# First group of an input projection: x's first tiles by another queue, products in the order of their parts

## The chip, the cores and the metric

One core of a Trainium2 chip. The metric is the device time of one execution in microseconds (us), the median of several runs. TensorE (PE) multiplies 128x128 weights with up to 512 columns into PSUM; ScalarE (ACT) and VectorE (DVE) work elementwise; GpSimd (POOL) sets a few constants; SyncE (SP) issues transfers. Each engine executes its own instructions in order and waits on semaphores for the others.

## What is computed

One decoder layer on x of 256 tokens by 1024: a root-mean-square norm, one input projection into queries, keys and values of two head groups, block attention and gated linear attention (GLA) on them, an output projection, a gated convolutional feed-forward block, and a last norm. The part around the change is the first of the projections, GLA's q and k and the 16 columns of its gate:

```python
xn = rms_norm(x, attn_norm_g[l])
proj = xn @ w_in[l]
...
gq = split_heads(proj[..., o_gq:o_gk], GLA_HEADS)
gk = split_heads(proj[..., o_gk:o_gv], GLA_HEADS)
gate_lr = proj[..., o_gg:]
log_a = jax.nn.log_sigmoid((gate_lr @ w_gate_up[l] + b_gate[l]).astype(jnp.float32)) / GLA_GATE_TAU
```

The norm's factor of a token is applied behind the products, so the products start from x itself.

## The kernel before, in words

Every 32-bit product is made of three products of split numbers: each operand is a high part (hi, rounded to the matmul's type) and a low part (lo, the rest), and hi·hi, hi·lo and lo·hi are added up (`mm3`, lines 108 to 111). ScalarE makes a high part (`split_hi`, L92), VectorE the low part from it (`split_lo`, L95). For x the two are `ah` and `al` (`xsplit`, L169 and L170); for weights `hi` and `lo`.

Weights come in slots. A slot is a tile `raw` that a transfer fills (four buffers), and a pair hi and lo (three buffers each). The low part that ends a slot calls `load_next`, which issues the next slot's transfer into the buffer just freed. Slots 0 to 3 hold the first group's weights, two depth steps k of 528 columns each; slots 4 and up hold 512 columns for four depth steps.

The input projection runs over 48 steps q: group g = q // 8 and depth step k = q % 8. Group 0 (G, q = 0 to 7) is GLA's q, k and gate columns: 256 tokens in two halves tt, 528 columns in two parts (272 and 256, one PSUM bank each), three products: 12 a step, 96 in all, lines 658 to 667. Group 1 and 2 (q, k of the attention) have 12 products of 256 columns a step.

Which work stands at which step is a plan: `on(q, f)` puts f ahead of step q's products (lines 558 to 626). TensorE's order is the written one. ScalarE's and VectorE's instructions are put in order by the scheduler, by what it expects to be ready first. In the plan `xsplit(k)` stands at q = k-1; the squares of x (`xsq`, L232) and their sum (`xadd`, `xsum`) at q = 1 to 8; the norm's factor (`xnorm`, L246 on TensorE, then Ln and Exp, L177 and L178) at q = 8; its row (`xrow`, L254), the evacuation of group 0 (`g_evac`, L262 and L263) and the split of the gate columns (`g_lr_split`) at 10; transposes (L282, L291) at 11; the gate's products (L311) at 12; its decay at 14; the gate's weights (`g_wgs`, L268 and L270) at 8. Slot 1's and later slots' splits start up to seven steps ahead of their use.

All of x and the weights are issued by SP, in this order: x k=0, slot 0 in three parts with x k=1 behind the second, x k=2, slot 1's half, x k=3, slot 1's other half, x k=4-5, slot 2, x k=6-7, slot 3. Small constants (wgu, ident, par, cos, sin) are issued at q = 1 to 4 among the later slots' transfers.

Ahead of the first product TensorE runs six warming products of zeros (L73, each two instructions), and ScalarE loads its function table (L54).

Of the kernel before, what the change touches and what calls it, by code (L numbers as in the profile page):

```python
# [9 lines left out]
F32 = mybir.dt.float32  # L10
# [8 lines left out]
HM, HD = 8, 64  # L19
HG, DK, DV = 4, 64, 128  # L20
RANK = 16
WARM = 6
TAU = 16.0
DFF = 2816
NP = DFF // 128
# [9 lines left out]
def trunk_kernel(ctx: ExitStack, tc: tile.TileContext, xT_d, wG_d, w5_d, wo_d, up_d, dn_d,  # L35
# [15 lines left out]
        return ps_att.tile([128, 512], F32, name="att")  # L51


    A.preload_act_table_set("natural_log_exp_and_others")  # L54
    par = const.tile([128, NPAR], F32, name="par")
    cos = const.tile([128, S], F32, name="cos")
    sin = const.tile([128, S], F32, name="sin")
# [11 lines left out]
    warm = const.tile([128, 128], F32, name="warm")  # L69
    V.memset(warm, 0.0)  # L70
    wp = att()
    for _ in range(WARM):
        T.matmul(wp[:, :128], warm, warm, start=True, stop=True)  # L73


    RAW, SPL = 4, 3
# [55 lines left out]
    def load_next():  # L132
        if nload[0] < len(items):
            items[nload[0]].load()
            nload[0] += 1
# [9 lines left out]
    rsx = main.tile([128, 8], F32, name="rsx")  # L145

    slots[0].raw = ring.tile([128, 2048], F32, name="raw", bufs=RAW)
    def load_x(k0, k1):
        a, b = (KT + S * k0 if k0 else 0), KT + S * k1
        DMA.dma_start(xg[:, a:b], xT_d[:, a:b])  # L150

    load_x(0, 1)
    for a, b in ((0, 272), (272, NG), (NG, 2 * NG)):
        DMA.dma_start(slots[0].raw[:, a:b], slots[0].src[:, a:b])
        if b == NG:
            load_x(1, 2)
    nload[0] = 1
    load_x(2, 3)
    slots[1].raw = ring.tile([128, 2048], F32, name="raw", bufs=RAW)
    DMA.dma_start(slots[1].raw[:, :NG], slots[1].src[:, :NG])  # L160
    load_x(3, 4)
    DMA.dma_start(slots[1].raw[:, NG:2 * NG], slots[1].src[:, NG:])
    nload[0] = 2
    for s in range(2, 4):
        load_x(2 * s, 2 * s + 2)
        load_next()

    def xsplit(k):
        A.activation(ah[:, k], xT[:, k], AF.Copy, scale=pag[:, k:k + 1])  # L169
        V.scalar_tensor_tensor(al[:, k], xT[:, k], pag[:, k:k + 1], ah[:, k],  # L170
                               op0=ALU.mult, op1=ALU.subtract)
# [59 lines left out]
    def xsq(n):  # L231
        A.activation(xsqs[:, 2 * n:2 * n + 2], xT[:, 2 * n:2 * n + 2], AF.Square)  # L232
# [325 lines left out]
    def on(q, f, *a):  # L558
        plan.setdefault(q, []).append((f, a))

    for k in range(1, KT):
        on(k - 1, xsplit, k)
    for dst, src, q in ((wgu, wgu_d, 1), (ident, ident_d, 1), (par, par_d, 3), (cos, cos_d, 4),
                        (sin, sin_d, 4), (lvl, lvl_d, 10), (causal, causal_d, 14), (glag, gla_g_d, 24)):
        on(q, DMA.dma_start, dst, src)
    for n in range(4):
        on(2 * n + 1, xsq, n)
        if n:
            on(2 * n + 1, xadd, n)
    on(8, xsum)  # L570
    on(8, xnorm)
    on(10, xrow)
    for tt in range(2):
        on(16, rope_a, 0, tt)
        on(24, rope_a, 1, tt)
    on(10, g_evac, 0)
    on(10, g_evac, 1)
    on(8, g_wgs)
    on(10, g_lr_split)
    on(11, g_transpose_lr)  # L580
    on(11, g_transpose, 0)
    on(11, g_transpose, 1)
    on(16, g_diag)
    on(12, g_gate_mm)
    on(12, g_gate)
    on(14, g_decay)
    on(15, lvl_u, 0)
    on(19, lvl_u, 1)
    on(24, lvl_first)
# [26 lines left out]
    for tt in range(2):  # L616
        on(53 + tt, g_out, tt)

    for n, sl in enumerate(slots[1:], 1):
        q0 = first_use[n]  # L620
        qa = max(0, q0 - 7)
        if n >= SPL:
            qa = max(qa, first_use[n - SPL + 1])
        on(qa, sl.alloc)
        on(qa, sl.split, 0, sl.n // 2)
        on(qa + (3 if q0 - qa > 4 else 1), sl.split, sl.n // 2, sl.n)

    slots[0].alloc()
    xsplit(0)
    for a, b in ((0, 272), (272, NG), (NG, 2 * NG)):  # L630
        slots[0].split(a, b)

    def emit(q):
        for f, a in plan.get(q, []):
            f(*a)

    names = ["G", "q", "k", "v", "gv", "r"]
    for q in range(48):
        g, k = divmod(q, 8)
        emit(q)  # L640
        if k == 0:
            if g == 0:
                st["G"] = [(acc(), att()) for _ in range(2)]
            else:
                st[names[g]] = [acc() for _ in range(2)]
        if g == 0:
            h_, l_ = slots[k // 2].view(NG)
            kk = k % 2
        else:
            h_, l_ = slots[4 + 2 * (g - 1) + k // 4].view(512)  # L650
            kk = k % 4
        if g in (1, 2):
            for pr in range(4):
                cs = slice(pr * 128, pr * 128 + 128)
                mm3(st[names[g]][pr // 2][:, (pr % 2) * S:(pr % 2 + 1) * S], h_[:, kk, cs], l_[:, kk, cs],
                    ah[:, k], al[:, k], k == 0 and pr % 2 == 0, k == KT - 1, skip_group_check=True)
            continue
        for tt in range(2):
            sh = ah[:, k, tt * 128:(tt + 1) * 128]
            sl = al[:, k, tt * 128:(tt + 1) * 128]  # L660
            if g == 0:
                a, b = st["G"][tt]
                parts = ((a[:, :272], 0, 272), (b[:, :256], 272, 528))
            else:
                parts = ((st[names[g]][tt], 0, 512),)
            for o, c0, c1 in parts:
                mm3(o, sh, sl, h_[:, kk, c0:c1], l_[:, kk, c0:c1], k == 0, k == KT - 1)


    hh_ = main.tile([128, KT, S], F32R, name="hh", tag="ah")  # L670
# [385 lines left out]
```

## Time and profile before

| | us |
|---|---|
| median of 3 runs | 314.3 (314.22 to 314.69) |
| profiled execution, its own time | 314.39 |
| its span, first to last instruction | 311.8 |
| TensorE busy | 304.9 (98%) |
| VectorE busy | 246.0 (79%) |
| ScalarE busy | 201.5 (65%) |
| first to last product of the first group | 4.18 to 19.19 |

The profile is of one execution, with times from the start of its span. A product's duration is modelled and overlaps its neighbour's, so the distance from start to start is what to read. Idle time in a row is what its engine stood still ahead of it, and behind the arrow is what ended that. L92 is line 92 of the kernel.

### The profile page before, as it was taken

The page shows a single profiled execution, that of the slowest core. Times are in us where ns is not written, and L with a number is a line of the kernel's source. Part 1 is how long each engine was busy: PE and PEld are TensorE (multiplying, and loading weights), DVE is VectorE, ACT ScalarE, POOL GpSimd, SP SyncE. Part 2 cuts the span into 40 slices and gives each one's busy share as a digit, 9 for nine tenths or more (in the row PEclk, how much of TensorE's full clock was granted, in tenths as well). Part 3 has the DMA queues.
Part 4 walks back from the last instruction along what each step waited for, and adds up shares of the span by engine and source line. Part 5 has one row for each costly group of instructions (what it writes and reads, how often), then busy time and mean ns, then how long its engine had stood idle before and what let it go on. Part 6 is the DMA issues. An engine that isn't in the chain of part 4 may idle for free.

```text
span 311.8 us, 6135 instructions
## 1 busy us (share of the span) xinstructions
PE 304.9 (98%) x2458; PEld 282.9 (91%) x2458; DVE 246.0 (79%) x464; ACT 201.5 (65%) x367; POOL 1.8 (1%) x12
## 2 busy tenths in 40 slices
PE   8999999999999999999999999999999999999992
PEld 7999997776788999999999999999999999999982
DVE  3996989897747497999999878888777777776653
ACT  5989997588866486466766655566666555534362
POOL 1000000000000000000000000000000000000000
PEclk9999999999999999999999999999999999999999
DMA  6998733734430615694566654445455722220003
GB/s 185 386 407 326 297 131 154 271 111 161 137 137 24 246 41 193 229 372 181 203 212 232 266 210 172 163 183 193 195 203 204 269 67 69 67 69 0 2 0 135
DMA packets 12443, 55.38 MB, mean 178 GB/s; under 512 B 1392, under 2 KB 3200, under 8 KB 8064
## 3 DMA queue, kind: packets, MB, share of 16 engines
q1 hardware_dynamic: 12272, 54.75, 47.5%
q8 instruction: 19, 0.31, 0.4%
q10 hardware_dynamic: 144, 0.26, 0.2%
q14 instruction: 8, 0.07, 0.1%
HBM read 53.95 MB, written 1.05 MB: 176 GB/s over the span
## 4 chain that ended last, share of the span: by engine, by line
PE 96%; DMA 1%; ACT 1%; DVE 0%; SPq 0%; issue 0%; DVEq 0%; ACTq 0%
PE acc L109 15%; PE acc L110 15%; PE acc L111 15%; PE att L110 15%; PE att L109 15%; PE att L111 15%; DMA xg<-in_xT 1%; PE att L377 1%; PE att L536 1%; PE att L506 1%; PE att L548 1%; PE att L439 1%; PE acc L816 0%; PE att L437 0%; PE att L470 0%; PE att L549 0%
## 5 line engine op out<-in xcount | busy, mean ns | idle before, releaser
L92 ACT ACTIVATE hi<-raw 128x1024 fp32r<-128x1024 f32 (+3 forms) x84 | 79.7, 973 | 51.0 <-PE att L110 43.2
L95 DVE TENSOR_TENSOR lo<-raw,hi 128x1024 fp32r<-128x1024 f32 (+3 forms) x86 | 93.6, 1099 | 12.6 <-ACT hi L92 12.5
L109 PE MATMUL att<-hh,hi 128*128 128x256 f32 x352 | 98.5, 280 | 0.0
L111 PE MATMUL att<-hh,lo 128*128 128x256 f32 x352 | 98.4, 279 | 0.0
L110 PE MATMUL att<-hl,hi 128*128 128x256 f32 x352 | 98.3, 279 | 0.0
L109 PEld LDWEIGHTS att<-hh,hi 128*128 128x128 f32 x352 | 66.2, 188 | 0.0
L111 PEld LDWEIGHTS att<-hh,lo 128*128 128x128 f32 x352 | 66.2, 188 | 0.0
L110 PEld LDWEIGHTS att<-hl,hi 128*128 128x128 f32 x352 | 66.2, 188 | 0.0
L782 DVE SCALAR_TENSOR_TENSOR c<-us,par,c 128x256 f32<-128x256 f32 x88 | 40.7, 482 | 4.1 <-ACT c L774 2.5
L774 ACT ACTIVATE c<-us,par 128x256 f32<-128x256 f32 x44 | 24.0, 591 | 21.5 <-DVE us L764 16.0
L111 PE MATMUL acc<-dhi,gl 128*128 128x512 f32 (+1 forms) x88 | 32.3, 367 | 0.0
L110 PE MATMUL acc<-dlo,gh 128*128 128x512 f32 (+1 forms) x88 | 32.2, 366 | 0.0
L109 PE MATMUL acc<-dhi,gh 128*128 128x512 f32 (+1 forms) x88 | 31.8, 361 | 0.0
L721 DVE TENSOR_TENSOR dlo<-draw,dhi 128x1024 fp32r<-128x1024 f32 x22 | 26.6, 1219 | 0.0
L764 DVE TENSOR_TENSOR us<-att,rb 128x512 f32<-128x512 f32 x20 | 13.8, 689 | 15.9 <-PE att L111 15.9
L109 PE MATMUL acc<-hi,ah 128*128 128x512 f32 (+1 forms) x64 | 25.6, 400 | 0.2 <-ACT hi L92 0.2
L110 PE MATMUL acc<-lo,ah 128*128 128x512 f32 (+1 forms) x64 | 24.6, 384 | 0.1
L111 PE MATMUL acc<-hi,al 128*128 128x512 f32 (+1 forms) x64 | 24.2, 378 | 0.0
L716 ACT ACTIVATE dhi<-draw 128x1024 fp32r<-128x1024 f32 x22 | 23.1, 1048 | 0.0
L110 PEld LDWEIGHTS acc<-dlo,gh 128*128 128x128 f32 x88 | 16.5, 188 | 3.0
L109 PEld LDWEIGHTS acc<-dhi,gh 128*128 128x128 f32 x88 | 16.6, 188 | 2.9
L111 PEld LDWEIGHTS acc<-dhi,gl 128*128 128x128 f32 x88 | 16.5, 188 | 2.6
(202 smaller groups left out, 517.3 us busy)
## 6 DMA issues: line engine op xcount, KB each, us to landing
raw<-in_up SPq DMA_DIRECT2D x22, 1024.0 KB, 4.8
draw<-in_dn SPq DMA_DIRECT2D x22, 512.0 KB, 5.7
raw<-in_w SPq DMA_DIRECT2D x8, 1024.0 KB, 6.8
raw<-in_wo SPq DMA_DIRECT2D x4, 1024.0 KB, 4.8
raw<-in_w SPq DMA_DIRECT2D x4, 512.0 KB, 7.3
raw<-in_wG SPq DMA_DIRECT2D x2, 528.0 KB, 6.9
raw<-in_wG SPq DMA_DIRECT2D x3, 264.0 KB, 4.3
xg<-in_xT SPq DMA_DIRECT2D x2, 256.0 KB, 6.0
```

The source lines that it names most:

```text
L92: A.activation(self.hi[:, a:b], self.raw[:, a:b], AF.Copy)
L95: V.tensor_sub(self.lo[:, a:b], self.raw[:, a:b], self.hi[:, a:b])
L109: T.matmul(out, sh, mh, start=first, stop=False, **kw)
L110: T.matmul(out, sh, ml, start=False, stop=False, **kw)
L111: T.matmul(out, sl, mh, start=False, stop=last, **kw)
L377: T.matmul(p[h][64 * j:64 * j + 64, c + 32 * g:c + 32 * g + 32], k[ps, a:a + 64], q, start=True, stop=True)
L439: T.matmul(o, AT[:, i], gv[:, tt, vs], start=(tt == 0), stop=True)
L716: A.activation(hi, downs[i][0], AF.Copy)
L721: V.tensor_sub(lo, d, hi)
L764: V.tensor_tensor(u[:, :, 2:], upo[i][2].rearrange("p (a t) -> p a t", a=2), rb[:, None, :].to_broadcast([128, 2, S]), op=ALU.mult)
L774: A.activation(cv[i][:, a], u[:, a, 2:], AF.Identity, bias=par[:, P_CB + m:P_CB + m + 1], scale=par[:, P_CW + 2 * 2 * NP + m:P_CW + 2 * 2 ...
L782: V.scalar_tensor_tensor(c[:, a], u[:, a, w:w + S], par[:, wc:wc + 1], c[:, a], op0=ALU.mult, op1=ALU.add)
```

## The change

ScalarE's queue issues x of k=0 and k=1 and loads the table behind them; SP issues the weights of slot 0 at once and then whole pairs of x and whole slots, the constants behind slot 3. VectorE copies the first 272 columns of the first high part. From there to q = 14 ScalarE's and VectorE's instructions stand in the written order. A step's twelve products of the first group go by part: four hi·ah, four hi·al, four lo·ah. Norm, row, transposes and gate stand up to one step later, wgs at 11; there are seven warming products.

```diff
-WARM = 6
+WARM = 7
...
-    A.preload_act_table_set("natural_log_exp_and_others")
...
+    with tc.manual_schedule(engines={mybir.EngineType.Activation}):
+        load_x(A, 0, 1)
+        load_x(A, 1, 2)
+        A.preload_act_table_set("natural_log_exp_and_others")
     for a, b in ((0, 272), (272, NG), (NG, 2 * NG)):
         DMA.dma_start(slots[0].raw[:, a:b], slots[0].src[:, a:b])
-        if b == NG:
-            load_x(1, 2)
     nload[0] = 1
-    load_x(2, 3)
-    slots[1].raw = ring.tile([128, 2048], F32, name="raw", bufs=RAW)
-    DMA.dma_start(slots[1].raw[:, :NG], slots[1].src[:, :NG])
-    load_x(3, 4)
-    DMA.dma_start(slots[1].raw[:, NG:2 * NG], slots[1].src[:, NG:])
...
+    load_x(DMA, 2, 4)
+    load_next()
+    load_x(DMA, 4, 6)
+    load_next()
+    load_x(DMA, 6, 8)
+    load_next()
+    for dst, src in ((ident, ident_d), (cos, cos_d), (sin, sin_d), (par, par_d), (wgu, wgu_d)):
+        DMA.dma_start(dst, src)
...
+    first = ExitStack()
+    first.enter_context(tc.manual_schedule(engines={mybir.EngineType.Activation, mybir.EngineType.DVE}))
+
+    def gsplit(k):
+        sl, a = slots[k // 2], NG * (k % 2)
+        if k % 2 == 0:
+            sl.alloc()
+        xsplit(k)
+        if k == 1:
+            xsq(0)
+        sl.split(a, a + NG)
+
     slots[0].alloc()
+    V.tensor_copy(slots[0].hi[:, :272], slots[0].raw[:, :272])
     xsplit(0)
-    for a, b in ((0, 272), (272, NG), (NG, 2 * NG)):
-        slots[0].split(a, b)
+    slots[0].split_hi(272, NG)
+    slots[0].split_lo(0, 272)
+    slots[0].split_lo(272, NG)
+    for k in range(1, 5):
+        gsplit(k)
+    xsq(1)
+    gsplit(5)
+
+    def first_group(q):
+        if q == 2:
+            gsplit(6)
+            xsq(2)
+            xadd(1)
+            gsplit(7)
+            xsq(3)
+            xadd(2)
+        elif q == 4:
+            slots[4].alloc()
+            slots[4].split(0, 1024)
+            xadd(3)
+            xsum()
+            slots[4].split(1024, 2048)
+        elif q == 6:
+            slots[5].alloc()
+            slots[5].split_hi(0, 1024)
+            slots[5].split_hi(1024, 2048)
+        elif q == 9:
+            xnorm()
+            slots[5].split_lo(0, 1024)
+            g_evac(0)
+            g_evac(1)
+            g_lr_split()
+            slots[6].alloc()
+            slots[6].split_hi(0, 1024)
+            slots[5].split_lo(1024, 2048)
+        elif q == 11:
+            xrow()
+            g_wgs()
+        elif q == 12:
+            g_transpose_lr()
+            g_transpose(0)
+            g_transpose(1)
+            slots[6].split_hi(1024, 2048)
+            slots[6].split_lo(0, 1024)
+        elif q == 13:
+            g_gate_mm()
+            g_gate()
+        elif q == 14:
+            g_decay()
+            slots[6].split_lo(1024, 2048)
+            first.close()
...
         emit(q)
+        first_group(q)
...
+        if g == 0:
+            for n, (mov, sta) in enumerate(((h_, ah), (h_, al), (l_, ah))):
+                for c, (c0, c1) in enumerate(((0, 272), (272, 528))):
+                    for tt in range(2):
+                        T.matmul(st["G"][tt][c][:, :c1 - c0], sta[:, k, tt * 128:(tt + 1) * 128],
+                                 mov[:, kk, c0:c1], start=k == 0 and n == 0, stop=k == KT - 1 and n == 2)
+            continue
```

The plan's lines for what `first_group` now calls are taken out, and the plan's loop over slots starts at slot 7.

## Rows read from the trace of the kernel before

**Rows 1.** The page of the profile: the line of busy time by engine (busy us, share of the span, instructions; PE is TensorE's products, PEld its weight loads), and the shares by engine in the chain of work that ended last.

```profile
PE 304.9 (98%) x2458; PEld 282.9 (91%) x2458; DVE 246.0 (79%) x464; ACT 201.5 (65%) x367; POOL 1.8 (1%) x12
...
PE 96%; DMA 1%; ACT 1%; DVE 0%; SPq 0%; issue 0%; DVEq 0%; ACTq 0%
```

**Rows 2.** Busy time by stretch, the long middle of the span. Columns: stretch and its length, busy us and instructions of TensorE, its weight loads, VectorE, ScalarE and GpSimd, then the granted TensorE clock, the DMA engines' mean share and GB/s.

```profile
30.00:300.00 270.00, 270.00 (x2220) 249.68 (x2220) 219.71 (x409) 171.67 (x310) 0.32 (x3) 1.00 0.45 164
```

**Rows 3.** The same view for the last 36 products of the first group.

```profile
14.81:19.19 4.38, 4.38 (x38) 4.38 (x37) 4.38 (x7) 4.19 (x7) 0.00 (x0) 1.00 1.07 420
```

**Rows 4.** TensorE's products in order of time, 0 to 10.5 us. Columns: start us, duration us, engine, line, operation, output <- inputs, shapes, count, and in brackets the idle time before and what ended it.

```profile
1.05 2.93 PE L73 MATMUL att<-warm 128*128 128x128 f32 x12 [1.05 <-DVE warm L70]
4.18 0.60 PE L109 MATMUL acc<-hi,ah 128*128 128x272 f32 x1 [0.20 <-ACT hi L92]
4.73 0.59 PE L110 MATMUL acc<-lo,ah 128*128 128x272 f32 x1
...
5.35 0.41 PE L109 MATMUL att<-hi,ah 128*128 128x256 f32 x1
...
6.44 0.43 PE L111 MATMUL acc<-hi,al 128*128 128x272 f32 x1
...
7.31 0.50 PE L109 MATMUL acc<-hi,ah 128*128 128x272 f32 x1
7.96 0.60 PE L110 MATMUL acc<-lo,ah 128*128 128x272 f32 x1
...
9.90 0.35 PE L109 MATMUL att<-hi,ah 128*128 128x256 f32 x1
```

**Rows 5.** ScalarE in order of time, the same columns: the start of the span, and its late table load and its one issue of a transfer. Two hi in one row start half the way apart (12.91 - 11.83 is two of them).

```profile
3.30 0.51 ACT L169 ACTIVATE ah<-xg 128x256 fp32r<-128x256 f32 x1 [1.29 <-DMA xg<-in_xT]
...
11.83 1.18 ACT L92 ACTIVATE hi<-raw 128x528 fp32r<-128x528 f32 x2
12.91 0.89 ACT L169 ACTIVATE ah<-xg 128x256 fp32r<-128x256 f32 x2
13.71 0.62 ACT L232 ACTIVATE xsqs<-xg 128x512 f32<-128x512 f32 x1
...
20.42 0.26 ACT L177 ACTIVATE rsx<-att,eps 128x2 f32<-128x2 f32 x1 [1.05 <-DVE rsx L176]
...
299.15 1.28 ACT L948 ACT_TABLE_LOAD   x1
300.75 0.60 ACT L974 ACTIVATE jk<-acc 128x512 f32<-128x512 f32 x1 [0.32 <-PE acc L111]
...
308.43 0.39 ACTq L994 DMA_DIRECT2D out_y<-yy  x1
```

**Rows 6.** SP's queue in order of time: its fifth issue, and the two of slot 5 (x2: two issues in one row).

```profile
2.57 0.43 SPq L154 DMA_DIRECT2D raw<-in_wG  x1
...
11.34 0.81 SPq L85 DMA_DIRECT2D raw<-in_w  x2
```

**Rows 7.** Transfers by issue: destination <- source, queue, number, KB, us from the start of the issue to landing. In order, those issued at 0.73 (x, k=0), 3.52 and 4.47 (slot 1, k=2 and k=3), 5.42 (slot 2, whole), 7.93 and 8.36 (slot 4's halves) and 11.8 (slot 5's second half). Slot 3's stood at 6.37.

```profile
xg<-in_xT SPq DMA_DIRECT2D x1, 132.0 KB, 2.5
...
raw<-in_wG SPq DMA_DIRECT2D x1, 264.0 KB, 4.3
...
raw<-in_wG SPq DMA_DIRECT2D x1, 264.0 KB, 5.1
...
raw<-in_wG SPq DMA_DIRECT2D x1, 528.0 KB, 6.4
...
raw<-in_w SPq DMA_DIRECT2D x1, 512.0 KB, 7.2
...
raw<-in_w SPq DMA_DIRECT2D x1, 512.0 KB, 8.2
...
raw<-in_w SPq DMA_DIRECT2D x1, 512.0 KB, 7.4
```

**Rows 8.** VectorE in order of time.

```profile
4.24 0.77 DVE L95 TENSOR_TENSOR lo<-raw,hi 128x272 fp32r<-128x272 f32 x2
...
11.22 0.88 DVE L170 SCALAR_TENSOR_TENSOR al<-xg,ah 128x256 fp32r<-128x256 f32 x2
...
12.62 1.32 DVE L95 TENSOR_TENSOR lo<-raw,hi 128x528 fp32r<-128x528 f32 x2
...
16.82 1.22 DVE L95 TENSOR_TENSOR lo<-raw,hi 128x1024 fp32r<-128x1024 f32 x1
...
23.35 0.20 DVE L276 CAST lrs<-gqk 128x64 fp32r<-128x64 f32 x1 [0.22 <-ACT gqk L262]
```

**Rows 9.** Busy time by stretch again, for the DMA engines (the last two columns).

```profile
6.50:8.00 1.50, 1.35 (x7) 1.04 (x6) 0.93 (x3) 1.20 (x4) 0.00 (x0) 1.00 0.65 195
...
10.00:12.00 2.00, 2.00 (x18) 2.00 (x18) 2.00 (x4) 2.00 (x5) 0.00 (x0) 1.00 1.03 411
```

**Rows 10.** TensorE's products behind the first group: the norm, the product after it, and the transposes.

```profile
19.19 0.50 PE L246 MATMUL att<-ones,s 128*128 128x1 f32 x4
19.55 0.36 PE L109 MATMUL acc<-ah,hi 128*128 128x256 f32 x1
...
24.29 0.38 PE L282 MATMUL att<-ident,lrs 128*128 128x128 f32 x2
24.51 1.04 PE L291 MATMUL att<-ident,gqk 128*128 128x128 f32 x8
```

More of the change, by code (lines that the diff above doesn't have):

```diff
@@ L71, in trunk_kernel, with warming @@
     wp = att()
-    for _ in range(WARM):
-        T.matmul(wp[:, :128], warm, warm, start=True, stop=True)
+    def warming(n, w):
+        for _ in range(n):
+            T.matmul(wp[:, :w], warm, warm[:, :w], start=True, stop=True)
+    warming(WARM, 128)
     RAW, SPL = 4, 3
@@ L147, in trunk_kernel, with load_x @@
     slots[0].raw = ring.tile([128, 2048], F32, name="raw", bufs=RAW)
-    def load_x(k0, k1):
+    def load_x(q, k0, k1):
         a, b = (KT + S * k0 if k0 else 0), KT + S * k1
-        DMA.dma_start(xg[:, a:b], xT_d[:, a:b])
-    load_x(0, 1)
+        q.dma_start(xg[:, a:b], xT_d[:, a:b])
+    with tc.manual_schedule(engines={mybir.EngineType.Activation}):
+        load_x(A, 0, 1)
+        load_x(A, 1, 2)
+        A.preload_act_table_set("natural_log_exp_and_others")
     for a, b in ((0, 272), (272, NG), (NG, 2 * NG)):
         DMA.dma_start(slots[0].raw[:, a:b], slots[0].src[:, a:b])
-        if b == NG:
-            load_x(1, 2)
     nload[0] = 1
-    load_x(2, 3)
-    slots[1].raw = ring.tile([128, 2048], F32, name="raw", bufs=RAW)
-    DMA.dma_start(slots[1].raw[:, :NG], slots[1].src[:, :NG])
-    load_x(3, 4)
-    DMA.dma_start(slots[1].raw[:, NG:2 * NG], slots[1].src[:, NG:])
[L163 to L166, printed above, removed]
+    load_x(DMA, 2, 4)
[6 more added lines that the diff above has]
+        DMA.dma_start(dst, src)
     def xsplit(k):
@@ L559, in on @@
         plan.setdefault(q, []).append((f, a))
[L561 to L564, printed above, removed]
+    for dst, src, q in ((lvl, lvl_d, 10), (causal, causal_d, 14), (glag, gla_g_d, 24)):
         on(q, DMA.dma_start, dst, src)
[L566 to L572, printed above, removed]
     for tt in range(2):
@@ L575, in trunk_kernel @@
         on(24, rope_a, 1, tt)
[L576 to L582, printed above, removed]
     on(16, g_diag)
-    on(12, g_gate_mm)
-    on(12, g_gate)
-    on(14, g_decay)
     on(15, lvl_u, 0)
@@ L617, in trunk_kernel @@
         on(53 + tt, g_out, tt)
-    for n, sl in enumerate(slots[1:], 1):
+    for n, sl in enumerate(slots[7:], 7):
         q0 = first_use[n]
@@ L660, in trunk_kernel @@
             sl = al[:, k, tt * 128:(tt + 1) * 128]
[L661 to L667, printed above, removed]
+            mm3(st[names[g]][tt], sh, sl, h_[:, kk], l_[:, kk], k == 0, k == KT - 1)
     hh_ = main.tile([128, KT, S], F32R, name="hh", tag="ah")
```

## The prediction

> **What bounds the kernel now.** I read four views, in this order. The page's summary [rows 1] says TensorE is the end: it is busy 98% of the span and holds 96% of the chain that ended last. A share over the whole span does not say where time can be had, so next the stretches: between 30 and 300 us TensorE is busy all 270.00 of 270.00 us [rows 2]. Nothing there waits, so TensorE's products simply follow one another, and what is saved ahead of them moves the end by the same amount. That leaves the start. There the reader is to see three losses [rows 3, 4]: first a stretch of the group at its best pace, then its products one by one. First, the products of the first group (8 depth steps k of 12 products, 96 in all) run from 4.18 us to 19.19, where the norm's follow [rows 4, 10], 15.01 us, while the last 36 of them take 4.38 us, 0.1217 us each; at that pace 96 would take 11.7 us. Second, holes: product 2 comes 0.55 us after product 1, because it wants the low part of the weights, and at k=1 product 2 comes 0.65 us after product 1 for the same reason (idle before, released by VectorE's lo). Third, the pace: from 5.35 to 6.44 us five steps take 1.09 us, 0.218 us each, and the change to 0.12 comes near 9.9 us. 256 columns at 1.2 and 2.4 GHz are 0.213 and 0.107 us, so these are the two levels of the clock; the granted-clock column reads 1.00 already there and does not show it, the products' spacing does. Before the rise TensorE had run warming products from 1.05 us, then the first group with its two holes.
>
> **The terms, part by part.** The sum is made against the profiled execution: span 311.8 us, own time 314.39, so 2.6 us lie around the span; it is 0.09 us above the median 314.30.
>
> *Seven warming products.* Six are 12 instructions from 1.05 us; they end at 3.98 with the last lasting 0.43, so 0.23 us each [rows 4]. Fourteen hold TensorE until 1.05 + 14 x 0.23 = 4.27. The first product in the written order needs only ah of k=0 and the first 272 columns of hi. ah: x's first tile lands 2.5 us after its issue and ScalarE takes 0.51 [rows 5, 7], so 0.73 + 2.5 + 0.1 + 0.51 = 3.8, as before. hi: the weights are now SP's first issue, land about then too, and VectorE copies them; no row shows a copy of 272 columns, the bounds are the CAST of 64 columns, 0.20, and the subtraction of 272, half of 0.77 [rows 8]; with 0.3 it is there at 3.6. Both lie under the warming, which now sets the first product: 4.27, **0.09 later** than before.
>
> *x by ScalarE's queue, table load behind it.* ScalarE's only row of an issue lasts 0.39 us, and SP's fifth issue stood at 2.57 [rows 5, 6], so that one comes every 0.46. So ScalarE issues x0 at 0.73, x1 at 1.17, loads the table from 1.6 to 2.9, and x0 lands at 3.2: cost nothing, covered by that landing; without this cover up to 1.7 us of ah0. The late table load lasts 1.28 us, and the next ACTIVATE starts 0.32 us after it, with a matmul named as its releaser [rows 5]. The Trainium skill ("ScalarE: Activation LUTs", What ACT_TABLE_LOAD costs) says otherwise: 1.28 us and then some 1.38 us of drain, 2.66 in all. By that rule ah0 would start at 4.3 and the first product at 4.85; the late row disagrees, 1.60 us from the load's start to the next instruction.
>
> *Written order in parts.* Per k the four hi.ah products come first, then four hi.al, then four lo.ah: lo is wanted eight products after hi, not one. lo of k=0 is there by 5.0, wanted at 4.27 + 8 x 0.218 = 6.0. So both holes go. Weight loads do not increase: every product has a load of its own already [rows 1].
>
> *DMA order.* SP now issues w0 in two parts, w1, x2-3, slot 1 whole, x4-5, slot 2, x6-7, slot 3, then five constants: slot 1 fifth, at 2.57 instead of 3.52 and 4.47, slot 3 ninth, at 4.47 instead of 6.37 [rows 6, 7]. What becomes late next is k=2, which wants slot 1. In the kernel before the last 264 KB of slot 1 were 5.1 us in flight, its first 264 KB 4.3, and slot 2's 528 KB 6.4 [rows 7]; so slot 1 lands between 6.9 and 9.0. I take 7.9, near the row with the same 1,572 KB issued up to it (2.57 + 5.1 = 7.7). hi of k=2 is then out at 7.9 + 0.1 + 0.64 = 8.65. The Trainium skill ("DMA: Bandwidth & Descriptors", Issuing engines are not separate DMA queues) says that a second issuing engine saves only issue time. By this rule x1 wins nothing but its two places in SP's queue; the sum counts no more than that, though the DMA engines stood at 0.65 busy from 6.5 to 8.0 us before [rows 9], when SP had issued everything up to slot 3.
>
> *When the clock rises* no row of before can say for another stream of products. Bounds: the start of before's unbroken products, 5.1 us, and the same moment, 9.9. The stream is now unbroken from 1.05 on, and 5.1 is a bound without a rise in any row, so I take a moment past the middle, nearer to 9.9: **8.0**.
>
> *The first group.* From 4.27 to 8.0 at 0.218 are 17.1 products; the other 78.9 at 0.1217 take 9.60 us: end **17.6** instead of 19.19, 1.59 us earlier. k=2 starts at 8.0 + 6.9 x 0.1217 = 8.84, after 8.65: no hole. The other engines keep up: per pair of k ScalarE wants 1.08 for two hi, 0.80 for two ah and 0.62 for the squares, 2.5 us, and VectorE 0.88 for two al, 1.32 for two lo and as much as one lo for adding the squares, 2.9 at most, since neighbours overlap [rows 5, 8], against 24 x 0.1217 = 2.9.
>
> *Behind it, in written order.* Three thin covers. Slot 4's lo: ScalarE works through from hi of k=2 at 8.0 to hi of slot 4 at about 16.0, VectorE subtracts, 1.22 [rows 8], until 17.3; wanted at 17.9. Constants now travel ahead of slot 4: 64 + 128 + 128 + 93 + 16 = 429 KB by their tiles, at 411 GB/s [rows 9] about 1.0 us. Slot 4's halves landed at 7.9 + 7.2 = 15.1 and 8.4 + 8.2 = 16.6 [rows 7]; 1.9 sooner with slot 3 and 1.0 later makes 14.3 and 15.7, and ScalarE comes to them at 15.0 and 16.0. The norm and the gate: Ln now stands behind the high part of slot 5's second half in ScalarE's queue. That half landed at 11.8 + 7.4 = 19.2 before [rows 6, 7]; the stream is 1.9 us ahead and has 349 KB more in front, as wgu and ident went ahead of it already (0.9 us), so 18.2; its high part lasts 1.0, and Ln starts at 19.5. From Ln to the transposes it took 24.29 - 20.42 = 3.87 us [rows 5, 10]: 23.4. TensorE comes there at 17.6 + 4 x 12 x 0.1217 + 2 x 0.36 (the norm, 19.19 to 19.55, and the row taken alike) = 24.2. The gate's weights wgs: ScalarE ends the evacuations at 22.7, slot 6's high part at 23.7 and its two copies at 24.5; VectorE has a low part until 24.6, cos and sin and two subtractions of some 0.4 each: 26.2. TensorE wants them after the transposes (1.2 us) and twelve products, at 26.8. From both sides the three are 0 to 0.5 us, no gain being possible behind a TensorE that is not kept waiting; I take **0.1**. Nothing else gets longer: the norm, row, transposes and gate are the same instructions a step later.
>
> **Sum:** -1.59 + 0.1 = -1.5 us; 314.39 - 1.5 - 0.09 = **312.8**. Its own range: clock at 6.5 with slot 1 at 6.9 ends the group at 4.27 + 2.23 + 85.8 x 0.1217 = 16.9, 312.0; clock at 9 ends it at 18.0, 313.3.
>
> **The rivals.**
> *A. The clock rises at the same moment, 9.9.* Then 25.8 products go at the slow pace and the group ends at 18.4: only holes are won, -0.65, 313.65. For it: nothing in the trace ties the rise to the holes. Against: the products ran unbroken in before only from 5.1 on, now from the start.
> *B. Slot 1 as one transfer lands at 9.0* (slot 2's 6.4 us) or as late as slot 1 was whole before, 9.57. k=2 then starts at 9.7 or 10.3 and the group ends at 18.5 to 19.1: 313.7 to 314.2, no change. For it: halves became a whole and share the engines with more bytes; against: issued 0.95 and 1.9 us sooner.
> *C. Slower: ScalarE's written order.* Ln, the evacuations and the gate wait behind a high part that waits for slot 5's second half. It decides from a landing of 19.2 on (19.2 + 0.1 + 1.0 + 3.87 = 24.2); each us later costs one, and past 21.3 the 1.5 are gone and 0.6 more: 315 to 316. For it: before, ScalarE's order was not fixed and a late high part could be stepped over; against: 18.2 by the landings.
> *D. The table load holds ScalarE as the page says:* first product 0.6 us later, the group that much later: 313.4. The late row speaks against it.
>
> **Numbers.** A change of 0.2%, 0.63 us, is about the least that can be told here (the three runs spread over 0.47); faster means under 313.67. Forecast 0.56, A 0.22 (half of it on either side of that line), B 0.11 (mostly no change), C 0.08, D 0.03. Faster 0.56 + 0.11 + 0.03 + 0.02 = 0.72, same 0.20, slower 0.08. The range leaves out C and the far ends of B and of the early clock: 311.9 to 313.9.
>
> **What would show it.** Right: first product at 4.2 to 4.4 with no idle TensorE before it; eight products of k=0 and k=1 without a wait for lo; spacing falling to 0.12 before 9.0; slot 1 landing near 7.9; last product of the first group near 17.6; TensorE busy throughout from 30 on. Wrong: spacing of 0.22 until 9.9 (A); a wait of TensorE at k=2 for hi, released by a transfer (B); TensorE waiting at the transposes or the gate products for evacuations whose ScalarE queue waits on slot 5 (C); ah0 after 4.0 without a late landing (D). If the first group ends near 17.6 and the time does not follow, then the later stretch was not as tight as it looks.

## The result: slower by 2.2 us

The kernel after takes 316.4 us (median of 8 runs, 315.15 to 318.02); the one before, beside it, 314.24 (8 runs). The ratio is 1.0071, 95% interval 1.0054 to 1.0088: slower, and 2.5 us above the upper end of the range, 313.9. The profiled execution took 316.94 with a span of 315.2, so 1.74 us lie around the span, where before had 2.59. The span alone grew by 3.4 us, and the time around it fell by 0.85. The three longest of the eight executions (317.06 to 318.02) are those with the lowest mean granted clock, 0.993 to 0.994 against 0.998 in the other five (315.15 to 316.94), and the profile shown is of one of the five; four executions lie at 315.15 to 315.86 and four at 316.94 and above, with the median between them.

### The profile page after: what moved, and what is told of

Same layout as the page of the kernel before. It is cut to its first block, busy times and chain, and to the rows that moved or that the text cites. A ratio compares the mean times of both kernels' runs of the same rounds, so it can differ in the third digit from the quotient of the medians.

```text
span 315.2 us, 6135 instructions
## 1 busy us (share of the span) xinstructions
PE 305.4 (97%) x2460; PEld 283.5 (90%) x2460; DVE 246.7 (78%) x465; ACT 201.7 (64%) x366; POOL 1.8 (1%) x12
## 4 chain that ended last, share of the span: by engine, by line
PE 94%; ACT 2%; DMA 1%; DVE 1%; issue 0%; DVEq 0%; SPq 0%; ACTq 0%
PE acc L112 14%; PE att L114 14%; PE att L113 14%; PE att L112 14%; PE acc L114 14%; PE acc L113 14%; PE att L713 2%; PE acc L713 2%; DMA raw<-in_wG 1%; PE att L381 1%; PE att L540 1%; PE att L510 1%; ACT qs L487 1%; PE att L552 1%; PE att L443 1%; PE acc L868 0%
## 5 line engine op out<-in xcount | busy, mean ns | idle before, releaser
L114 PE MATMUL acc<-ah,lo 128*128 128x256 f32 x64 | 18.0, 281 | 2.5 <-DVE lo L98 2.5
L112 PE MATMUL acc<-hi,ah 128*128 128x512 f32 x48 | 20.2, 421 | 0.0
L114 PE MATMUL acc<-hi,al 128*128 128x512 f32 x48 | 19.0, 396 | 0.0
L113 PE MATMUL acc<-lo,ah 128*128 128x512 f32 x48 | 19.0, 396 | 0.0
```

What stands on the lines that cost most here:

```text
L112: T.matmul(out, sh, mh, start=first, stop=False, **kw)
L113: T.matmul(out, sh, ml, start=False, stop=False, **kw)
L114: T.matmul(out, sl, mh, start=False, stop=last, **kw)
```

## The profile after

First the page's line of busy time by engine and the shares of the chain that ended last, then the stretch 30 to 300 us; they answer to [rows 1, 2].

```profile
PE 305.4 (97%) x2460; PEld 283.5 (90%) x2460; DVE 246.7 (78%) x465; ACT 201.7 (64%) x366; POOL 1.8 (1%) x12
...
PE 94%; ACT 2%; DMA 1%; DVE 1%; issue 0%; DVEq 0%; SPq 0%; ACTq 0%
```

```profile
30.00:300.00 270.00, 267.53 (x2212) 247.85 (x2211) 220.04 (x408) 172.98 (x311) 0.31 (x3) 1.00 0.46 166
```

TensorE now stands still for 2.47 us of a stretch where it never did. TensorE's products in order of time show where (answers to [rows 4, 10]).

```profile
1.05 3.35 PE L74 MATMUL att<-warm 128*128 128x128 f32 x14 [1.05 <-DVE warm L69]
4.43 0.82 PE L713 MATMUL acc<-hi,ah 128*128 128x272 f32 x2
5.41 0.79 PE L713 MATMUL att<-hi,ah 128*128 128x256 f32 x2 [0.15 <-ACT hi L95]
...
9.52 0.66 PE L713 MATMUL acc<-lo,ah 128*128 128x272 f32 x2
9.97 0.52 PE L713 MATMUL att<-lo,ah 128*128 128x256 f32 x2
10.33 0.41 PE L713 MATMUL acc<-hi,ah 128*128 128x272 f32 x2
...
18.85 0.40 PE L713 MATMUL att<-lo,ah 128*128 128x256 f32 x2
20.48 0.50 PE L250 MATMUL att<-ones,s 128*128 128x1 f32 x4
24.27 0.68 PE L258 MATMUL att<-ident,rsx 128*128 128x128 f32 x4 [0.37 <-issue]
28.80 0.47 PE L315 MATMUL att<-lrT,wgs 128*128 128x256 f32 x2
...
38.97 0.38 PE L114 MATMUL acc<-ah,lo 128*128 128x256 f32 x1 [2.47 <-DVE lo L98]
```

The holes for lo are gone, but a row of two products still takes 0.45 us until 9.97: the clock rose at 10.0, as in before. The group ends at 19.08, 0.11 us sooner than [rows 4, 10]. The first GLA block's products, at 43.91 before, stand at 47.33: 3.4 us are lost between the two points, and nothing after. The rows show 0.37 and 2.47 us of it as idle of TensorE. SP's queue shows the first reason (answers to [rows 6]; the last row holds the two halves of slot 4, of slot 5, and three more).

```profile
3.87 0.33 SPq L88 DMA_DIRECT2D raw<-in_wG  x1
...
7.50 0.33 SPq L170 DMA_DIRECT2D sin<-in_sin  x1
8.88 0.33 SPq L170 DMA_DIRECT2D par<-in_par  x1
9.54 0.34 SPq L170 DMA_DIRECT2D wgu<-in_wgu  x1
10.97 10.27 SPq L88 DMA_DIRECT2D raw<-in_w  x7
```

Slot 1, issued at 2.58, was 6.3 us in flight and landed at 8.88, when `par` was issued; slot 2, issued at 3.87, was 7.0 in flight and landed at 10.87, and slot 4 went out at 10.97. SP waits for the oldest transfer: eight are in flight (ScalarE's two counted in), and an issue goes out when the eighth before it has landed. Slot 4 is issued 3.0 us later than in before (7.93), and slot 5's second half lands at 13.4 + 8.7 = 22.1. ScalarE in order of time (answers to [rows 5]):

```profile
0.73 0.89 ACTq L153 DMA_DIRECT2D xg<-in_xT  x2
1.66 1.28 ACT L159 ACT_TABLE_LOAD   x1 [1.66 <-PEq L1097]
3.87 0.51 ACT L173 ACTIVATE ah<-xg 128x256 fp32r<-128x256 f32 x1 [0.93 <-DMA xg<-in_xT]
...
22.14 1.06 ACT L95 ACTIVATE hi<-raw 128x1024 fp32r<-128x1024 f32 x1 [1.56 <-DMA raw<-in_w]
23.10 0.24 ACT L181 ACTIVATE rsx<-att,eps 128x2 f32<-128x2 f32 x1
```

The Ln at 23.10 stood at 20.42: it waits behind that high part. TensorE pays 0.37 us of it at 24.27. Last, VectorE ahead of the long wait:

```profile
33.45 1.22 DVE L98 TENSOR_TENSOR lo<-raw,hi 128x1024 fp32r<-128x1024 f32 x1
34.58 0.48 DVE L326 TENSOR_SCALAR d<-att,par 128x256 f32<-128x256 f32 x1
36.43 0.69 DVE L494 TENSOR_TENSOR mqT<-acc,cos 128x512 f32<-128x512 f32 x1 [1.37 <-ACT qs L487]
37.08 0.69 DVE L334 TENSOR_TENSOR d<-d,e 128x512 f32<-128x512 f32 x1
37.69 1.22 DVE L98 TENSOR_TENSOR lo<-raw,hi 128x1024 fp32r<-128x1024 f32 x1
```

The low part at 37.69 is slot 6's second. In the written order of q = 14 it stands behind `g_decay`, whose L334 needs ScalarE's e. TensorE wanted it at 36.5. Work of rope, which stands outside the written part, is slipped in on both engines. The row of VectorE shows 1.37 us of waiting at rope's mqT, but that wait cost next to nothing by itself: e was ready only at 36.42 + 0.63 = 37.05. ScalarE in order of time shows what held e up:

```profile
34.53 0.59 ACT L487 ACTIVATE qs<-acc 32x512 f32<-32x512 f32 x1
35.14 0.64 ACT L328 ACTIVATE e<-e 128x512 f32<-128x512 f32 x1
35.80 0.59 ACT L487 ACTIVATE qs<-acc 32x512 f32<-32x512 f32 x1
36.42 0.63 ACT L329 ACTIVATE e<-e 128x512 f32<-128x512 f32 x1
```

Two copies of rope (qs) stand ahead of the gate's last two steps, 0.6 us each.

## The experiments

Theory O: the loss is the written order, above all this low part. Rivals: the five constants up front (slots late), the clock, Ln behind slot 5. All times are medians; ratios are to the kernel before on the same chip.

| | us | ratio, 95% interval |
|---|---|---|
| 1 low part ahead of the gate | 314.46 | 1.0008 (0.9998 to 1.0017) |
| 2 constants later | 315.12 | 1.0028 (1.0017 to 1.0039) |
| 3 both | 315.9 | 1.0055 (1.0042 to 1.0067) |
| 4 before + order of parts | 313.87 | 0.9987 (0.9974 to 0.9999) |
| 5 before + x by ScalarE | 313.11 | 0.9970 (0.9959 to 0.9981) |
| 6 before + constants up front | 315.57 | 1.0052 (1.0039 to 1.0065) |
| 7 as 1, Ln ahead | 313.97 | 0.9992 (0.9983 to 1.0000) |
| 8 as 4 and 5 | 312.87 | 0.9961 (0.9949 to 0.9972) |
| 9 as 7, constants in steps | 316.28 | 1.0067 (1.0051 to 1.0082) |
| 10 as 8, seven warming | 312.85 | 0.9954 (0.9938 to 0.9970) |
| 11 as 8, first hi on VectorE | 313.01 | 0.9962 (0.9947 to 0.9976) |
| 12 as 7, constants by GpSimd | 315.22 | 1.0023 (1.0009 to 1.0037) |
| 13 as 12, behind slot 2 | 314.29 | 0.9997 (0.9983 to 1.0012) |
| 14 after without written order | 313.25 | 0.9977 (0.9961 to 0.9992) |
| 15 as 1, again | 314.6 | 1.0005 (0.9994 to 1.0017) |
| 16 as 7, again | 314.09 | 0.9992 (0.9983 to 1.0000) |

**1, the low part.**

```diff
         elif q == 13:
+            slots[6].split_lo(1024, 2048)
             g_gate_mm()
...
             g_decay()
-            slots[6].split_lo(1024, 2048)
```

> The changed kernel with one line moved: slot 6's second low part stands ahead of the gate on VectorE instead of behind its decay. Theory O (that line alone makes TensorE wait 2.47 us at 38.97): the wait goes, 316.4 - 2.5 = 313.9 us. Theory Q (SP's queue issues slots 4 to 6 late, the gate chain is late and drags everything behind it): the high part or another low part is late next, at most 0.5 us comes back, 316.

314.46: 1.9 of the 2.2 us are back (theory O expected 2.5, Q at most 0.5), and the wait at 38.97 is gone. In its place two smaller waits appear that after does not have, 0.8 us in all, for the softmax's e (`pe`):

```profile
62.70 0.55 PE L540 MATMUL att<-ident,pe 128*128 128x128 f32 x3 [0.31 <-ACT pe L532]
...
75.51 0.55 PE L540 MATMUL att<-ident,pe 128*128 128x128 f32 x3 [0.48 <-ACT pe L532]
```

**2 and 3, the constants among the later slots**, alone and with 1.

```diff
-    for dst, src in ((ident, ident_d), (cos, cos_d), (sin, sin_d), (par, par_d), (wgu, wgu_d)):
-        DMA.dma_start(dst, src)
...
     gsplit(1)
+    DMA.dma_start(wgu, wgu_d)
+    DMA.dma_start(ident, ident_d)
...
     gsplit(5)
+    DMA.dma_start(par, par_d)
...
             xadd(2)
+            DMA.dma_start(cos, cos_d)
+            DMA.dma_start(sin, sin_d)
```

> The changed kernel with the five constants back behind the transfers of slots 4 to 7, so that slot 4 is issued when its buffer is free (near 8 us, not 10.97). Theory Q: slot 5's second half lands near 19 instead of 22.1, Ln starts at 20.5 to 21 instead of 23.1, TensorE loses none of the 1.0 us between 20 and 30 and the decay comes earlier, so part or all of the 2.47 us goes too: 313 to 315.4. Theory O: only the 1.0 us, 315.4, with a wait for slot 6's low part of 2 us or more left.

> The changed kernel with both edits. O and Q together: TensorE waits nowhere after the first group, whose end (19.1 after, 19.2 before) then decides: span 311.7, and with 1.7 us around the span, as in the changed kernel, 313.5; with 2.6 us, as before, 314.3. If either theory is wrong, a wait of over 0.5 us stays between 20 and 40.

315.12 alone: theory Q's range, and against theory O, which expected a wait of 2 us or more to stay. Only 0.62 us of it is left:

```profile
35.37 0.39 PE L114 MATMUL acc<-ah,lo 128*128 128x256 f32 x1 [0.62 <-DVE lo L98]
```

So the wait in after hangs on the constants in front of slot 4 as well as on the low part's place, though in this profile the clock also rose early, at the first product. With 1 it is 315.9: not additive. VectorE's later instructions, which the scheduler orders, stand in another order here. In the third, `gkT` of a level stands behind four softmax operations; VectorE in order of time, then TensorE:

```profile
57.89 0.42 DVE L354 TENSOR_TENSOR gqT<-gqT,dec 128x256 f32<-128x256 f32 x1
...
59.46 0.47 DVE L518 CUSTOM_DVE_ANT_0 att<-att,causal 128x256 f32<-128x256 f32 x1
...
59.91 0.42 DVE L355 TENSOR_TENSOR gkT<-gkT,dec 128x256 f32<-128x256 f32 x1
```

```profile
60.48 0.67 PE L379 MATMUL att<-gqT,gkT 64*64 64x32 f32 x32 [1.91 <-DVE mx L520]
...
62.23 0.63 PE L113 MATMUL acc<-lo,ah 128*128 128x512 f32 x1
```

The row names mx, which ended last; the product reads gqT and gkT, and that gkT had ended just before. 1.91 us of idle, and the products then come 0.43 us apart instead of 0.23 until 65.4. The stretch (TensorE's busy time, granted clock, DMA share, GB/s) says why: the clock had fallen to its lower level.

```profile
62.00:64.00 2.00, 2.00 (x6) 0.50 0.06 25
```

This explains the profiled execution only: its mean granted clock is 0.989, that of the other four 0.998, and they took 315.55 to 316.32 all the same. What makes those slow is not shown.

**4, the order of parts alone**, put into the kernel before.

```diff
+        if g == 0:
+            for n, (mov, sta) in enumerate(((h_, ah), (h_, al), (l_, ah))):
...
```

> The kernel before with one part of the change alone: the twelve products of a step of the first group in the order of their parts. If the holes for lo are real losses and the clock rises at 9.9 as before: the holes of 0.33, 0.17, 0.43 and 0.18 us at the slow pace become five products more before the rise, 5 x 0.12 = 0.6 us, and 0.15 at k=4: 313.6. If the rise comes sooner when the holes are gone: 313 or less. If hi or ah is late in place of lo: no change, 314.2.

313.87, a gain of 0.4, just clear of the noise, and no wait of TensorE after 30 us.

**5, x's first two tiles by ScalarE's queue alone**, put into the kernel before.

```diff
-    load_x(0, 1)
+    with tc.manual_schedule(engines={mybir.EngineType.Activation}):
+        A.dma_start(xg[:, :KT + S], xT_d[:, :KT + S])
+        A.dma_start(xg[:, KT + S:KT + 2 * S], xT_d[:, KT + S:KT + 2 * S])
+        A.preload_act_table_set("natural_log_exp_and_others")
```

> The kernel before with one part alone: x's first two tiles by ScalarE's queue, its table load behind them; SP then issues the three parts of slot 0 first. Theory L (the ten transfers of the start share the DMA engines, so moving a tile to another queue moves no landing that counts): x0 lands near 3.8 instead of 3.2 and the second part of slot 0 near 4.9 instead of 4.3, the first product stands at 4.3 to 4.5 (4.09 in the profiles before), x1 lands about 1 us sooner, and the time is 314.0 to 314.6, ratio 0.999 to 1.001. Rival P (the 1.5 us that the prediction took for the start, the x tiles being its first term): 313.3 or less. A third, T (the time around the span follows the table load, 1.75 us against 2.1 to 2.6): span unchanged near 311.8, own time 0.5 to 0.8 lower, 313.5.

313.11: 1.1 us won, where theory L expected nothing; rival P's range. The stretch 5 to 10 us, before and in this kernel (last two columns: DMA share and GB/s):

```profile
5.00:10.00 5.00, 4.85 (x21) 4.54 (x22) 2.80 (x7) 3.67 (x8) 0.00 (x0) 1.00 0.88 282
```

```profile
5.00:10.00 5.00, 5.00 (x28) 4.76 (x28) 4.22 (x9) 4.75 (x10) 0.00 (x0) 1.00 1.03 356
```

SP is two issues of 0.46 us ahead, 0.9 us; the engines move 26% more in this stretch, slot 4 is issued at 7.17 instead of 7.93 and the norm stands at 18.29 instead of 19.19. A landing that shares the engines comes later by itself (x0 3.1 us in flight, 2.5 before), but x1 lands at 5.06 instead of 5.60 and slot 4 is issued sooner. The time around the span fell too, from 2.59 to 1.8 us in the profiles. The medians of all executions say how the 1.1 us are made up: the span fell by only 0.4 (311.7 to 311.3) and the time around it by 0.6 (2.40 to 1.80). So the larger part is what theory T named, and not the start of the products; the profile's 0.9 at the norm is one pair of executions.

**6, the constants up front alone**, put into the kernel before.

```diff
-    for dst, src, q in ((wgu, wgu_d, 1), (ident, ident_d, 1), (par, par_d, 3), (cos, cos_d, 4),
-                        (sin, sin_d, 4), (lvl, lvl_d, 10),
+    for dst, src, q in ((lvl, lvl_d, 10),
...
+    for dst, src in ((ident, ident_d), (cos, cos_d), (sin, sin_d), (par, par_d), (wgu, wgu_d)):
+        DMA.dma_start(dst, src)
```

> The kernel before with one part alone: identity, cos, sin, the vector of parameters and the 16x256 weight issued by SP directly behind slot 3 instead of among steps 1 to 4. Theory Q (SP's queue holds eight transfers; the next issue waits for the oldest landing): slot 4's first load is issued near 11 us instead of 7.93, when slot 2's lands, and slot 5's second half lands 21 to 22.5. The scheduler orders ScalarE here, so the Ln of the norm should not stand behind slot 5: norm within 0.3 of 19.19 plus what the clock's rise moves, and the time 314.0 to 314.6. Rival Q2 (the late slots themselves cost, whoever orders ScalarE): hi parts of slot 4 wait for DMA, TensorE waits 0.5 to 1.5 us between 20 and 40, time 314.8 to 315.8. Rival B (bandwidth, no places): slot 4's issue stays at 8 to 8.5, time unchanged.

315.57, 1.3 us lost: the issue at 11.92 is theory Q's, the time rival Q2's. TensorE waits 1.06 us at 21.32, not for a high part as Q2 has it, but for slot 4's low part, which the scheduler now puts behind the norm's step on VectorE.

```profile
21.32 0.39 PE L111 MATMUL acc<-ah,lo 128*128 128x256 f32 x1 [1.06 <-DVE lo L95]
```

**7, Ln ahead of slot 5's second high part**, on top of 1.

```diff
             slots[5].split_hi(0, 1024)
-            slots[5].split_hi(1024, 2048)
...
             g_lr_split()
+            slots[5].split_hi(1024, 2048)
```

> The kernel after with slot 6's second low part ahead of the gate (as in the first experiment, 314.46), and besides the high part of slot 5's second half moved on ScalarE from ahead of the norm's Ln to behind the evictions of the first group; order on the other engines the same. Theory C (about 1 us was lost between 20 and 30 because Ln waited behind slot 5's landing): Ln at 20.5 to 21 instead of 23.1, gate's products near 26.5 to 27.5 instead of 28.3 to 28.8, and 0.6 to 1.0 us off the time: 313.5 to 313.9, ratio to the kernel before 0.997 to 0.999. Rival (those 1 us are made good later, since TensorE had products of the second group to run meanwhile; only its own idle counts, 0.4 us or less): 314.2 to 314.6, ratio 1.000 to 1.001.

**15 and 16** are 1 and 7 again, side by side.

> The first experiment again, beside its successor on one chip: 314.2 to 314.7; by the profiles TensorE then waits 0.8 us in all behind 60 us, for the softmax's high part.

> The seventh experiment again. Theory C (Ln behind slot 5's second high part costs 0.5): 0.3 to 0.7 below the run beside it. Rival (the 0.5 between the first and the seventh came from where the clock rose, 10.0 and 6.2 us in their profiles, and from the chip): within 0.25 of it.

313.97 against 314.46, and 314.09 against 314.6: 0.5 us both times, with intervals that overlap a little in each pair (only 15 and 16 ran on one chip). That is a little under the 0.6 to 1.0 of theory C in 7, and within it in 16. The profiles of 15 and 16 agree: at the row's products 15 waits 0.56 us, 16 not at all.

```profile
23.58 0.68 PE L258 MATMUL att<-ident,rsx 128*128 128x128 f32 x4 [0.56 <-issue]
```

**8, parts and x together (the diffs of 4 and 5); 10 and 11 on top of it.**

```diff
-WARM = 6
+WARM = 7
```

```diff
-        slots[0].split(a, b)
+        if a == 0:
+            V.tensor_copy(slots[0].hi[:, :b], slots[0].raw[:, :b])
+        else:
+            slots[0].split_hi(a, b)
+        slots[0].split_lo(a, b)
```

> The kernel before with the order of products by parts (alone: 313.87, ratio 0.9987) and x's first two tiles by ScalarE's queue. If the parts are additive: 313.87 plus what the tiles alone do (314.0 to 314.6 minus 314.25), so 313.6 to 314.2, ratio 0.998 to 1.000. If the order of parts can use x1's earlier landing (its low part is wanted later in a step, so the hi parts of steps 1 and 2 bound it at 7.0 and 9.0): 313.0 to 313.5. If its ScalarE order, shuffled by the scheduler, opens a wait later on: above 314.6.

> The kernel of the eighth experiment (parts and x's tiles, 312.87) with seven warming products in place of six: warming ends 4.4 instead of 3.98, the first product stands at 4.8 as before, since it waits for the high part on ScalarE. Theory W (a gap of 0.8 us ahead of the first product delays the clock's rise, which stood at 8.6): rise up to 0.5 to 2 us sooner, time 311.9 to 312.7. Rival (rise moves from execution to execution by itself, between 4.5 and 10 in the profiles so far, and the data bind where it is early): 312.6 to 313.1, ratio to before 0.9955 to 0.997.

> The kernel of the eighth experiment (312.87) with the first high part of 272 columns on VectorE: 0.30 us there at 3.67 beside ScalarE's high part of x, so the first product at 4.4 instead of 4.79, the second step's waits unchanged. If the start of the products decides (clock's rise follows it): 0.2 to 0.4 off, 312.4 to 312.7. Rival (the steps behind wait for their data, or the second part of slot 0 at 4.9 is waited for instead, as in the kernel after at 5.41): 312.8 to 313.1. If the order of later steps, which changes with it in the sixth stage, opens a wait: above 313.3.

312.87 for 8, the best version with 10, 1.3 us under before; 4 and 5 alone gave 0.4 and 1.1, so nearly additive, and under every range expected, since these took 5 at next to nothing. The seventh warming product (312.85) and the first high part on VectorE (313.01) change nothing that can be told.

**9, three repairs at once.** The edit is 7 with the constants put back into the plan.

```diff
-    for dst, src, q in ((lvl, lvl_d, 10),
+    for dst, src, q in ((wgu, wgu_d, 1), (ident, ident_d, 1), (par, par_d, 4), (cos, cos_d, 6),
+                        (sin, sin_d, 4), (lvl, lvl_d, 10),
```

> The kernel after with all three costs taken away: slot 6's second low part ahead of the gate, slot 5's second high part behind the evictions on ScalarE, and the five constants back among the steps (16x256 weight and identity at step 1, parameters and sin at 4, cos at 6). In this order VectorE has the fourth level's gkT ahead of the softmax; in the third experiment it stood behind it. Theory (the costs add: 1.9 for the low part, 0.5 for Ln, 1.35 for the constants, against 1.1 won by x's tiles and 0.4 by the order of parts): 316.4 less 3.75, so 312.3 to 313.1, ratio 0.994 to 0.997, slot 4 issued near 7 to 8 us, no wait of TensorE over 0.5 us after 30. Rival (moving the constants scrambles later steps whatever gkT's place, as in the third experiment): 314.5 to 316. A third: the constants cost nothing once Ln doesn't wait: 313.7 to 314.2, as in the seventh experiment.

316.28, a clear miss. `cos` now goes out at 20.18 and lands at 27.4; on VectorE the scheduler has the gate's weights behind the work on cos, so the gate's products wait 0.74 us at 29.25, and softmax costs 1.45 between 30 and 300 (268.55 busy).

**12 and 13, the constants off SP's queue, with the order of every computing engine as in 7.** In 12 GpSimd issues cos, sin, par and wgu at once; in 13 behind a copy of one column of slot 2.

```diff
+    with tc.manual_schedule(engines={mybir.EngineType.Pool}):
+        DMA.dma_start(ident, ident_d)
+        nc.gpsimd.tensor_copy(const.tile([128, 1], F32, name="tiny"), slots[2].raw[:, 1055:1056])
+        for dst, src in ((wgu, wgu_d), (par, par_d), (cos, cos_d), (sin, sin_d)):
+            nc.gpsimd.dma_start(dst, src)
```

> The kernel of the seventh experiment (313.97; low part ahead of the gate, Ln ahead of slot 5's second high part) with cos, sin, parameters and the 16x256 weight (365 KB) issued at the start by GpSimd's queue in place of SP's; the order of every computing engine is the same. Theory Q (the constants cost by holding places in SP's queue): slot 4 is issued at 8 to 9 us in place of 11.38 and lands 1 us or more earlier, norm at 19 to 19.8, time 312.7 to 313.3. Theory R (they cost by the time that the DMA engines spend on them ahead of slots 4 and 5, whichever queue brings them: in the kernel before and after 341 to 409 GB/s at a share near 1 from 10 to 20 us): slot 4 lands as in the seventh experiment or later, time 313.8 to 314.6.

> As the twelfth experiment, but GpSimd issues the four constants only behind a one-column copy that reads slot 2, so after about 11 us; again no other order changes. Theory R (the DMA time of the constants ahead of slots 4 and 5 is what costs, 1.35 us in the kernel before): slot 4 issued at 7.5 to 9 us, slot 5's second half lands 2 us earlier than in the seventh experiment, time 312.5 to 313.2, ratio 0.994 to 0.997. Theory Q (places alone): as the twelfth, 312.7 to 313.3, no difference between the two. Rival S (the 1.35 us of the sixth experiment came from the scheduler's other order, not from the constants): 313.7 to 314.3 in both.

13: 314.29, no better than 7. Slot 4 was issued at 7.76 instead of 11.38, and ScalarE had all of slot 5's first half by 18.7, but Ln came at 20.97 (21.04 in 7): `xnorm` stands at q = 9, and TensorE reaches it no sooner. So once Ln is out of the way, the constants up front cost nothing that shows here: rival S, for 13. 12, at 315.22, is outside every range; its profile loses at the start: x0 was 3.5 and the second part of slot 0 4.9 us in flight beside four more transfers, and TensorE waited 0.97 us at 6.60.

**14, the kernel after without its written order:** the diffs of 4, 5, 6, 10 and 11 together; ScalarE and VectorE by the scheduler.

> The kernel after without its written order: x's tiles by ScalarE, first high part on VectorE, products by parts, seven warming products and the constants up front, all put into the kernel before; ScalarE and VectorE are ordered by the scheduler. Theory W (the written order is what makes the change lose; the constants cost 1.35 as in the sixth experiment): 312.9 and 1.35, so 313.8 to 314.5, 2 us under the kernel after. Rival (the constants cost only in the order of the sixth experiment): 312.6 to 313.3. A third (the loss is in what the parts do together, whoever orders): 315.5 to 316.5.

313.25, 3.15 us under the kernel after, within the rival's range. TensorE is busy all 270.00 us from 30 to 300 again.

```profile
30.00:300.00 270.00, 270.00 (x2219) 249.84 (x2218) 219.34 (x407) 172.23 (x309) 0.31 (x3) 1.00 0.45 164
```

14 leaves out more than the written order: norm, row, transposes, gate and wgs stand at the steps of before, and SP issues x and slot 1 in the pieces of before. Together these carry the whole loss. Experiments 1 and 7 put 1.9 and 0.5 us of it on two places in the written order; the rest was not parted. The constants cost 1.06 us of idle at 19.20 in 14's profile, but only 0.24 in the time against 11.

## Why the prediction was wrong

**What lies behind the 3.15 us.** From 316.4, moving the low part gives 1.87 (mean of 1 and 15: 314.53), Ln 0.5 (mean of 7 and 16: 314.03), and the softmax waits that 16 still has and 14 has not, 0.8 (269.24 against 270.00 busy): 313.2, where 14 measures 313.25. That it closes to 0.05 is luck: after's median is known to about half a us, and the sum leaves out that 14 waits 1.06 us at 19.20, where 16 does not, and that the clock rose at different times. In the kernel after itself the last term does not show; it is uncovered once the low part is moved.

**The step that failed** is "Behind it, in written order": taken at 0.1 us, within 0 to 0.5; by experiment 14 it is 3.15, with the later steps and SP's whole pieces in it. The profiled executions, set against the sum, say the same: the group's end moved by -0.11 where the sum has -1.59, what follows it cost 3.5 where it has 0.1, and the time around the span fell by 0.85 where it has nothing. Its list of "three thin covers" left one out: slot 6's second low part, behind the decay. The prediction followed the written order as far as wgs and then took the rest as "the same instructions a step later". What an instruction waits for is not the same when it is put behind another that waits, and instructions outside the written part can still be slipped in between: rope's two copies on ScalarE, 0.6 us each, stood ahead of the gate's last steps.

**Ln.** Forecast 19.5, from a landing at 18.2; it came at 23.10, from 22.1. The landing was reckoned from bytes and "one issue every 0.46". In after that rate ended once eight transfers were in flight. It could have been read in before: ident was issued at 9.60, and slot 1's second part, eight issues ahead of it, landed at 4.47 + 5.1 = 9.57 [rows 7]. Five constants in front of slot 4 are five such waits. So rival C's condition came true, past 21.3, but its price did not: "each us later costs one" forgot that TensorE has the second group's products in between. It cost 0.5, and the result, 316.4, comes out near rival C's 315 to 316 only by the other loss.

**The clock** was taken at 8.0 and rose at 10.0: rival A, for this profile. It is no property of the change: in the eighteen profiles it rose between the first product (2, 3) and 10.5 us (12), and for one kernel at 9.9 (1) and near 5 (15, on another chip), with medians 0.14 apart. Where it rises early, a step waits for its high part (0.78 us at 9.33 in 15): 5 us of the clock bring the norm only 0.96 us forward (20.57 in 1, 19.61 in 15).

**First product:** forecast 4.27, measured 4.43; x0 was 3.1 us in flight, not the 2.5 of [rows 7], and slot 0's second part 3.7 (2.3 before), which made the new hole at 5.41. Slot 1: forecast 7.9, measured 8.88; rival B's 9.0, harmless while the clock was low. The group's end: forecast 17.6, measured 19.08. The clock's 2 us make 2 x (1 - 0.1217/0.218) = 0.88 of it; the late start and the first four products, 0.85 us over the slow pace, make 0.85 x 0.1217/0.218 = 0.47.

**Right:** both holes for lo went (4 alone: 0.4 us). The table load behind x cost nothing: ah0 waited 0.93 us for x after it, so rival D's drain did not show. The copy of 272 columns took 0.30, as estimated. A gain at the start moves the end about one for one: 8's profile has the norm 0.92 sooner and the end 1.1. Experiment 14 falls inside the range, at 313.25 against 312.8, but partly by luck: its median span, 311.3, is 1.1 above the 310.2 that the sum gives, and 1.91 us lie around it where the sum kept 2.6.

**The second queue.** The prediction gave x's two tiles no more than their two places in SP's order. In the profiles that held: two issues of 0.46 us are 0.9 us, and alone the tiles bring 0.9 us at the norm (5). By the medians the span gained 0.4, and the other 0.6 of the 1.1 us lie around the span, a term that the prediction did not have. The Trainium skill ("DMA: Bandwidth & Descriptors", Issuing engines are not separate DMA queues) says that transfers of all issuing engines interleave on the same 16 engines and that a second issuer saves only the time to issue. The runs agree: x0 and the second part of slot 0 land later side by side (3.1 and 3.3 us in flight in 5, 2.5 and 2.3 before), and the gain at the norm is no more than the issue time.

## What to carry to other kernels

Before fixing an order by hand, list for every instruction in it what waits in front of it on its engine, to the end of the fixed part and past it, and when its consumer wants the result; a cover left out can cost its whole wait (2.47 us here). Count the transfers in flight, not only issue rate and bytes. A scheduler's order changed here with small edits 20 to 40 us away, so undo parts one at a time and read the later waits too: two repairs together (3) were slower than either. And compare spans as well as times over all executions: part of a gain can lie around the span (5).

## What the runs showed of the hardware

- An issue of SP waited until the eighth transfer before it had landed (7.50, 8.88, 10.97 in after). ScalarE's two count among the eight: SP's seventh and ninth issue in after stood at 3.87 and 5.22, and x0 and x1 landed at 3.83 and 5.17.
- The clock's rise scattered from under 4.5 to 10.5 us between executions, and for one kernel from near 5 to 9.9.
- A wait of 2.47 us at 38.97 left the granted clock at 1.00 (after); one of 1.91 at 60.48 brought it to 0.50 between 62 and 64 (3). Why the shorter one did is open. Other executions of both kernels differ: the mean granted clock is 0.993 to 0.998 in after, 0.989 to 0.998 in 3.
- With x's first tiles issued by ScalarE and the table load behind them, 1.73 to 1.99 us lie around the span in every execution (own time less span); without, 2.06 to 2.60 (before, 4, 6). The medians are 1.76 to 1.97 and 2.37 to 2.47, so 0.4 to 0.7 us of what these kernels win lie outside the span. Which of the two parts does it was not tried apart.
